# Overflow bookkeeping off GpSimd, row stores issued by ScalarE, and two token parts in one matmul operand for experts of at most 64 slots

## The chip, the cores and the metric

The kernel runs on one core of one Trainium2 chip. The metric is the device time of one execution in microseconds; for the kernel before it is 2696.34 us, the median of three runs (2691.31 to 2696.85). Times in the profile are microseconds unless marked ns. Engines: PE is TensorE (its matmuls; PEld its weight loads), DVE is VectorE, ACT is ScalarE, POOL is GpSimd, SP is SyncE, whose queue issues most DMAs.

## What is computed

Two transformer blocks on 512 tokens of width 1024, in fp32. The second block ends in a mixture of experts, the only part that the change touches:

```python
def swiglu(x, w_gu, w_down):
    g, u = jnp.split(x @ w_gu, 2, axis=-1)
    return (jax.nn.silu(g) * u) @ w_down

def moe_ffn(x2d, w_router, router_bias, w_exp_gu, w_exp_down, w_sh_gu, w_sh_down):
    scores = jax.nn.sigmoid((x2d @ w_router).astype(jnp.float32))
    sel = scores + router_bias.astype(jnp.float32)
    ...
    _, top_idx = lax.top_k(sel, TOP_K)
    w = jnp.take_along_axis(scores, top_idx, axis=1)
    w = w / jnp.sum(w, axis=-1, keepdims=True) * ROUTED_SCALE
    ...
    def expert_block(args):
        tok, e = args
        return swiglu(x_pad[tok], w_exp_gu[e], w_exp_down[e])
    ...
    routed = jnp.zeros((T + 1, D), x2d.dtype).at[buf_tok].add(out)[:T]
    return routed + swiglu(x2d, w_sh_gu, w_sh_down)
```

There are 64 experts. Each has a gate-and-up weight of 1024x512 and a down weight of 256x1024, 3 MB together. One shared expert works on all tokens. A layer norm follows.

## The kernel before

**fp32 by parts.** An fp32 operand is split into a high part and the rest: `split` (L216) copies with rounding to fp32r on ACT and subtracts on DVE. A product takes three matmuls, `mm3` (L192 to L194): high by high, high by low, low by high. Weights are split the same way when they have landed: units of 128x2048, copy on ACT (`unit<-whole`, `unit<-unit`), subtraction on DVE.

**Routing.** `route` computes the router's scores on PE, a sigmoid on ACT (L1623), the choice of groups and of experts on DVE (L1625 to L1690), and each expert's list of tokens. The experts are then worked off by falling count, each with a fixed number of slots, its cap (`CAPS`): 34 experts have caps of 66 to 104, and the 30 last ones 64 or fewer (5 of 64, 9 of 60, 5 of 56, 6 of 52, 5 of 48). The token rows are copied by POOL into tiles `xr` (two buffers) and stored by SP to the DRAM tensor `xr_d`, four stores of 128 rows (L1532), from which the experts gather.

**The loop over experts.** Iteration e, in the order in which the code issues it: POOL gathers the rows of expert e+4 from `xr_d` (indirect DMA, L1833); the gate-and-up weights of e+1 are split; `up(e)` does 24 matmuls of 512 columns, then silu on ACT (L1859) and the product on DVE (L1860); the down weight of e is split; `turn(e+1)` transposes the gathered rows on PE (L1847, 8 transposes) and splits them into `gh` and `gl`; `down(e-1)` does 12 matmuls, then two scaled copies into `ey` on ACT (L1877, two buffers), and POOL adds `ey` to the rows of the DRAM tensor `acc_d` by an indirect DMA that accumulates (the scatter, L1879); SP issues the weight loads of later experts; `turn_mid(e)` transposes the product (L1865) and splits it into `ehh` and `ehl`. Slot lists for later experts are made between (L1779 to L1786). Each scatter waits for the one before, as both add to `acc_d`.

**Order of the instructions.** A scheduler that works from the data dependences and its own costs orders the instructions of each engine when the kernel is built; each engine then runs its list in order.

**Overflow.** An expert with more tokens than its cap gets further blocks after the loop. `overflow()` makes the list of those blocks and runs in steps, one in each iteration from e = 8 on: a row of cap bounds by 75 memsets on POOL (L1740), comparisons and a scan on DVE, and three lists, for which a tile `cs` is filled by an iota on POOL (L1753), then by copies on ACT.

## Time and profile before

| | |
|---|---|
| median of 3 runs | 2696.34 us |
| the profiled execution, its own time | 2697.15 us |
| its span in the trace | 2695.4 us |
| mean granted clock of TensorE, of full speed | 0.974 |
| PE busy | 2532.2 us, 94% |
| DVE busy | 1983.9 us, 74% |
| ACT busy | 1439.6 us, 53% |
| POOL busy | 497.7 us, 18% |
| read from and written to HBM | 405.70 MB and 41.60 MB |

The span is the time between the first and the last instruction in the trace; the run's own time holds a little more. The mixture of experts begins at about 1900 us: routing and the shared expert to about 1982, the experts with caps above 64 to about 2360, the others to about 2670, then the final layer norm. A busy share tells how much an engine does, not whether anything waits for it; the idle time in brackets behind an instruction of a timeline, with what ended it, tells that.

### The profile page before, as it was taken

To read this page: it belongs to the slowest core of one execution; us is meant where nothing else is said; L and a number is where in the kernel's file an instruction comes from. 1 tells how busy PE (TensorE), PEld (TensorE's weight loads), DVE (VectorE), ACT (ScalarE), POOL (GpSimd) and SP (SyncE) were. 2 spreads that over 40 slices of the span, in tenths; PEclk is the share of its full clock that TensorE was granted. 3 is DMA by queue.
4 is the path that set the end of the run, shared out by engine and by line. 5 is a ranking of instruction groups with operands and counts; after the bars stand their busy time and mean duration, and the time that the engine had idled before them with its cause. 6 is when DMAs were issued, how large, how long until landed. Compare 5 with 4: busy or idle time off the path is not lost. (4 is left out here: it accounts for less than half of the span.)

```text
span 2695.4 us, 33112 instructions
## 1 busy us (share of the span) xinstructions
PE 2532.2 (94%) x12188; PEld 1929.2 (72%) x12188; DVE 1983.9 (74%) x2921; ACT 1439.6 (53%) x1874; POOL 497.7 (18%) x606
## 2 busy tenths in 40 slices
PE   8999999999998888999999999999889899999995
PEld 6778878888887676888888777788666565555552
DVE  6987865763667985763756798757679788888885
ACT  6656443432433564432434566535348677777783
POOL 0212200000002210000000347000214344434332
PEclk9999999999999898999999999999889899999997
DMA  4334332323223101223224632533569999999994
GB/s 135 126 110 125 106 126 85 106 79 108 94 82 106 32 32 63 94 83 105 95 84 126 189 113 88 198 121 132 228 202 331 319 354 346 355 358 365 362 360 147
DMA packets 232969, 449.49 MB, mean 167 GB/s; under 512 B 23375, under 2 KB 172815, under 8 KB 207205
## 3 DMA queue, kind: packets, MB, share of 16 engines
q1 hardware_dynamic: 220677, 410.42, 44.4%
q0 software_dynamic: 12128, 36.94, 5.9%
q8 instruction: 97, 1.59, 0.2%
q14 instruction: 67, 0.55, 0.1%
HBM read 405.70 MB, written 41.60 MB: 166 GB/s over the span
## 5 line engine op out<-in xcount | busy, mean ns | idle before, releaser
L192 PE MATMUL acc<-xh,unit 128*128 128x512 f32 (+1 forms) x1584 | 623.9, 394 | 4.8 <-ACT unit L216 1.8
L193 PE MATMUL acc<-xl,unit 128*128 128x512 f32 (+1 forms) x1584 | 624.0, 394 | 0.0
L194 PE MATMUL acc<-xh,lower 128*128 128x512 f32 (+1 forms) x1576 | 620.1, 394 | 0.0
L216 DVE TENSOR_TENSOR lower<-whole,unit 128x2048 fp32r<-128x2048 f32 (+3 forms) x218 | 463.6, 2127 | 210.5 <-ACT unit L216 210.0
L216 ACT ACTIVATE unit<-whole 128x2048 fp32r<-128x2048 f32 (+3 forms) x223 | 397.3, 1782 | 345.8 <-DMA whole<-in_f_down_w_dram 116.2
L192 PEld LDWEIGHTS acc<-xh,unit 128*128 128x128 f32 (+1 forms) x1584 | 297.6, 188 | 69.1 <-ACT unit L216 2.3
L193 PEld LDWEIGHTS acc<-xl,unit 128*128 128x128 f32 (+1 forms) x1584 | 297.9, 188 | 62.3 <-DVE xl L276 0.6
L194 PEld LDWEIGHTS acc<-xh,lower 128*128 128x128 f32 (+1 forms) x1576 | 296.3, 188 | 62.9 <-issue 2.3
L216 DVE TENSOR_TENSOR unit<-unit 128x2048 fp32r<-128x2048 f32 x131 | 298.5, 2285 | 30.0 <-ACT unit L216 27.2
L216 ACT ACTIVATE unit<-unit 128x2048 fp32r<-128x2048 f32 x131 | 249.0, 1913 | 26.5 <-PE acc L194 9.1
L1879 POOL DMA_INDIRECT acc_d<-ey,idx x64 | 148.2, 2316 | 353.0 <-DMA acc_d<-ey,idx 77.5
L192 PE MATMUL acc<-unit,gh 128*60 128x512 f32 (+14 forms) x512 | 208.1, 406 | 3.1 <-ACT gh L216 1.9
L194 PE MATMUL acc<-unit,gl 128*60 128x512 f32 (+14 forms) x512 | 208.1, 406 | 1.7 <-DVE gl L216 1.6
L311 DVE SCALAR_TENSOR_TENSOR y<-u,vtab,y 128x510 f32<-128x510 f32 (+1 forms) x176 | 131.2, 749 | 29.7 <-ACT y L309 25.3
L194 PE MATMUL acc<-mh,lower 128*128 128x512 f32 x352 | 138.7, 394 | 0.0
L192 PE MATMUL acc<-mh,unit 128*128 128x512 f32 x352 | 138.7, 394 | 0.0
L193 PE MATMUL acc<-ml,unit 128*128 128x512 f32 x352 | 138.7, 394 | 0.0
L1833 POOL DMA_INDIRECT xg<-xr_d,idx x64 | 105.5, 1649 | 106.6 <-PE aux L1847 53.3
L624 DVE SCALAR_TENSOR_TENSOR cc<-gg,vtab,cc 128x512 f32<-128x512 f32 x148 | 119.9, 868 | 1.1 <-ACT cc L594 1.0
L193 PE MATMUL acc<-unit,gh 128*60 128x512 f32 (+14 forms) x288 | 116.8, 405 | 0.0
L192 PE MATMUL acc<-unit,ehh 128*60 128x512 f32 (+14 forms) x256 | 101.1, 408 | 12.5 <-ACT ehh L216 12.4
L1877 ACT ACTIVATE ey<-acc,slot 60x512 f32<-60x512 f32 (+13 forms) x128 | 84.1, 681 | 51.9 <-PE acc L194 23.4
(691 smaller groups left out, 4555.7 us busy)
## 6 DMA issues: line engine op xcount, KB each, us to landing
unit<-in_w_exp_gu_dram SPq DMA_DIRECT2D x72, 1024.0 KB
unit<-in_w_exp_down_dram SPq DMA_DIRECT2D x59, 1024.0 KB
whole<-in_w_exp_gu_dram SPq DMA_DIRECT2D x56, 1024.0 KB
whole<-in_f_up_w_dram SPq DMA_DIRECT2D x44, 1024.0 KB
whole<-in_a_in_proj_dram SPq DMA_DIRECT2D x16, 1024.0 KB
whole<-in_f_down_w_dram SPq DMA_DIRECT2D x16, 768.0 KB
whole<-in_b_pw_w_dram SPq DMA_DIRECT2D x12, 1024.0 KB
whole<-in_w_in_dram SPq DMA_DIRECT2D x12, 1024.0 KB
```

Of the source, the lines that this page charges most:

```text
L192: T.matmul(ps, lhsT=ah, rhs=bh, start=start, stop=False)
L193: T.matmul(ps, lhsT=ah, rhs=bl, start=False, stop=False)
L194: T.matmul(ps, lhsT=al, rhs=bh, start=False, stop=stop)
L216: return A.activation(out=xh, in_=x, func=AF.Copy), eng.tensor_sub(xl, x, xh.bitcast(F32))
L311: V.scalar_tensor_tensor(y[:, d:], in0=u[:, :S - d], scalar=vcol(cw, (2 - d) * 44 + j), in1=y[:, d:], op0=ALU.mult, op1=ALU.add)
L624: V.scalar_tensor_tensor(c, in0=gg[j][:, k:k + S], scalar=vcol("b_dw_w", k * KD + j), in1=c, op0=ALU.mult, op1=ALU.add)
L1833: self.gathered = G.indirect_dma_start(out=self.xg, out_offset=None, in_=xr_d, in_offset=IO(ap=self.idx, axis=0))
L1877: A.activation(out=y[:, n0:n0 + S], in_=ps, func=AF.Copy, scale=self.wgt)
L1879: G.indirect_dma_start(out=acc_d, out_offset=IO(ap=self.idx, axis=0), in_=y, in_offset=None, compute_op=ALU.add)
```

## The change

Three parts. (1) The four stores to `xr_d` are issued by ACT's queue and no longer by SP's. (2) `overflow()` uses no GpSimd step and no copies: the caps stand in a constant tile `caps`, filled by 15 memsets at the start of the kernel; adding the bound of a block and comparing go into one DVE operation for each of five blocks; the list of experts' numbers comes from the constants `irow` and `eids`, broadcast. (3) `gh` and `gl` become two places in one tile `gs`. For experts with cap at most 64, `gl` starts at column 64, and `up()` multiplies both at once: for each of the 8 slices of the inner dimension one matmul with 64+cap stationary columns against the high part of the weight and one with cap columns against the low part, 16 instead of 24. The result of the low tokens stands in the rows from 64 on; ACT copies it to a new tile `gx`, DVE adds the other rows to it, and silu and product read `gx`. Where cap is under 64 (25 experts), POOL clears the columns between.

```diff
@@ -1529,7 +1529,7 @@
                     xr = turned.tile([P, D], F32, name="xr", tag="gb", bufs=2)
                     G.tensor_copy(xr.rearrange("p (u k q) -> p u k q", u=2, k=4),
                                   xn[:, t, :].rearrange("p (u q k) -> p u k q", u=2, k=4))
-                    nc.sync.dma_start(out=xr_d[1 + t * P:1 + (t + 1) * P, :], in_=xr)
+                    nc.scalar.dma_start(out=xr_d[1 + t * P:1 + (t + 1) * P, :], in_=xr)
                 shared(rp, xn, acc_d, sh, last)
             dense.close()
             free_units[:] = [p for p in free_units if p is not wp]
@@ -1568,7 +1568,7 @@
                         for i, x in enumerate((a["ln3_g_2"], a["ln3_b_2"])):
                             nc.sync.dma_start(out=ln3[:, i * D:(i + 1) * D], in_=x[0].partition_broadcast(P))
                     if e >= OVERFLOW_AT:
-                        steps = steps or overflow(sp, mb, ob, pcol, eids, n_more, more, ex[e].gathered)
+                        steps = steps or overflow(sp, mb, ob, pcol, eids, n_more, more)
                         next(steps, None)
 
                 g3, b3 = (ln3[:, i:i + D] for i in (0, D))
@@ -1723,40 +1723,34 @@
                 V.tensor_sub(wm, wm, rr[:, :, :, i])
         return posm, rr, mb, ob, pcol, eids
 
-    def overflow(sp, mb, ob, pcol, eids, n_more, more, gathered):
+    def overflow(sp, mb, ob, pcol, eids, n_more, more):
 
         n = N_OVER * NE
-        room = sp.tile([P, 4 * n + P + 1], F32, name="room", bufs=1)
-        bv, fl, hit, cs = (room[:, i * n:(i + 1) * n] for i in range(4))
-        dg, lst = room[:, 4 * n:4 * n + P], room[:, 4 * n + P:4 * n + P + 1]
+        room = sp.tile([P, 3 * n + P + 1], F32, name="room", bufs=1)
+        fl, hit, cs = (room[:, i * n:(i + 1) * n] for i in range(3))
+        dg, lst = room[:, 3 * n:3 * n + P], room[:, 3 * n + P:3 * n + P + 1]
 
         def blocks(x):
             return x.rearrange("p (b e) -> p b e", e=NE)
 
-        with tc.issue_after(gathered.ins):
-            for e in range(NE):
-                if e == 0 or CAPS[e] != CAPS[e - 1]:
-                    for b in range(N_OVER):
-                        G.memset(blocks(bv)[:, b, e:], float(CAPS[e] + b * CAP))
         pc = aux([P, NE])
         for t in range(NT):
             T.matmul(pc, lhsT=ob, rhs=mb[:, t, :], start=t == 0, stop=t == NT - 1)
         for b in range(N_OVER):
-            V.tensor_tensor(blocks(fl)[:, b, :], blocks(bv)[:, b, :], pc, op=ALU.is_lt)
+            V.scalar_tensor_tensor(blocks(fl)[:, b, :], in0=caps, scalar=float(b * CAP), in1=pc, op0=ALU.add, op1=ALU.is_lt)
         yield
         V.tensor_scalar(hit, fl, 0.0, 1.0, op0=ALU.mult, op1=ALU.add)
         V.tensor_tensor_scan(cs, hit, fl, 0.0, op0=ALU.mult, op1=ALU.add)
         V.tensor_copy(n_more, cs[:, n - 1:])
         V.scalar_tensor_tensor(hit, in0=cs, scalar=pcol, in1=fl, op0=ALU.is_equal, op1=ALU.mult)
         for i in range(3):
-            if i == 0:
-                G.iota(blocks(cs), pattern=[[0, N_OVER], [1, NE]], base=0, channel_multiplier=0,
-                       allow_small_or_imprecise_dtypes=True)
-            if i == 1:
+            yield
+            if i < 2:
+                V.tensor_mul(blocks(fl), blocks(hit), (irow[:, :NE], eids)[i][:, None, :].to_broadcast([P, N_OVER, NE]))
+            else:
                 for b in range(N_OVER):
-                    copy(blocks(cs)[:, b, :], eids)
-            yield
-            V.tensor_mul(fl, bv if i == 2 else cs, hit)
+                    V.scalar_tensor_tensor(blocks(fl)[:, b, :], in0=caps, scalar=float(b * CAP), in1=blocks(hit)[:, b, :],
+                                           op0=ALU.add, op1=ALU.mult)
             V.reduce_sum(lst, fl, axis=AX.X)
             V.tensor_scalar(dg, ident, lst, None, op0=ALU.mult)
             yield
@@ -1765,6 +1759,10 @@
             V.tensor_copy(more[i], pl)
             yield
 
+    caps = const.tile([P, NE], F32, name="caps")
+    for e in range(NE):
+        if e == 0 or CAPS[e] != CAPS[e - 1]:
+            G.memset(caps[:, e:], float(CAPS[e]))
     irow = const.tile([P, P], F32, name="irow")
     G.iota(irow, pattern=[[1, P]], base=0, channel_multiplier=0, allow_small_or_imprecise_dtypes=True)
     pad = const.tile([P, 1], F32, name="pad")
@@ -1839,25 +1837,44 @@
             self.dn = cut(self.unit[2], self.turned)
 
         def turn(self):
-            self.gh = self.gp.tile([P, KD, CAP], F32R, name="gh", tag="gh", bufs=2)[:, :, :self.cap]
-            self.gl = self.gp.tile([P, KD, CAP], F32R, name="gl", tag="gl", bufs=2)[:, :, :self.cap]
+
+            cap = self.cap
+            self.wide = cap <= 64
+            at = 64 if self.wide else CAP
+            self.gs = self.gp.tile([P, KD, 2 * CAP], F32R, name="gs", tag="gs", bufs=2)
+            self.gh, self.gl = self.gs[:, :, :cap], self.gs[:, :, at:at + cap]
+            if self.wide and cap < 64:
+                G.memset(self.gs[:, :, cap:64].bitcast(F32), 0.0)
             for k4 in range(0, KD, 4):
-                pt = aux([P, 4, self.cap])
+                pt = aux([P, 4, cap])
                 for k in range(4):
-                    T.transpose(pt[:, k, :], self.xg[:, (k4 + k) * P:(k4 + k + 1) * P], ident[:self.cap, :self.cap])
+                    T.transpose(pt[:, k, :], self.xg[:, (k4 + k) * P:(k4 + k + 1) * P], ident[:cap, :cap])
                 self.turned = split(self.gh[:, k4:k4 + 4, :], self.gl[:, k4:k4 + 4, :], pt)
 
         def up(self):
-            ps = bank()[:self.cap]
+            cap = self.cap
+            ps = bank()
             for k in range(KD):
                 hi, lo = w = self.gu[k // 4]
-                mm3(ps, self.gh[:, k, :], self.gl[:, k, :], hi[:, k % 4, :], lo[:, k % 4, :], k == 0, k == KD - 1)
+                if self.wide:
+                    both = [(64 + cap, hi), (cap, lo)]
+                    for n, x in both if k == 0 else both[::-1]:
+                        T.matmul(ps[:n], lhsT=self.gs[:, k, :n], rhs=x[:, k % 4, :], start=k == 0 and x is hi,
+                                 stop=k == KD - 1 and x is hi)
+                else:
+                    mm3(ps[:cap], self.gh[:, k, :], self.gl[:, k, :], hi[:, k % 4, :], lo[:, k % 4, :], k == 0, k == KD - 1)
                 if k % 4 == 3:
                     free(w)
-            self.hx = self.sp.tile([CAP, 256], F32, name="hx", tag="hx", bufs=2)[:self.cap]
+            if self.wide:
+                x = self.sp.tile([64, S], F32, name="gx", tag="gx", bufs=1)[:cap]
+                copy(x, ps[64:64 + cap])
+                V.tensor_add(x, x, ps[:cap])
+            else:
+                x = ps[:cap]
+            self.hx = self.sp.tile([CAP, 256], F32, name="hx", tag="hx", bufs=2)[:cap]
             by_block = self.hx.rearrange("t (k p) -> t p k", k=2)
-            A.activation(out=by_block, in_=ps[:, 0:256].rearrange("t (p k) -> t p k", k=2), func=AF.Silu)
-            V.tensor_mul(by_block, by_block, ps[:, 256:512].rearrange("t (p k) -> t p k", k=2))
+            A.activation(out=by_block, in_=x[:, 0:256].rearrange("t (p k) -> t p k", k=2), func=AF.Silu)
+            V.tensor_mul(by_block, by_block, x[:, 256:512].rearrange("t (p k) -> t p k", k=2))
 
         def turn_mid(self):
             pt = aux([P, 2, self.cap])
```

What the scheduler makes of it, at two places. **Routing, ACT**, from the first copy of the router's sums (`rsc<-acc`) to the sigmoid (L1623 `rsc<-aux`); `unit<-whole` are weight copies for the shared expert and the first experts, `xh` the high part of the tokens. Before:

```order
L77 ACTIVATE rsc<-acc 64x256
L216 ACTIVATE xh<-aux 128x4x128 x2
L216 ACTIVATE unit<-whole_68 128x2048
L216 ACTIVATE unit<-whole_70 128x2048
L77 ACTIVATE rsc<-acc 64x256
L216 ACTIVATE unit<-whole_66 128x2048
L1623 ACT_TABLE_LOAD
L1623 ACTIVATE rsc<-aux 128x256
```

After:

```order
L77 ACTIVATE rsc<-acc 64x256
L1532 DMA xr_d<-xr 128x1024
L216 ACTIVATE xh<-aux 128x4x128 x2
L1532 DMA xr_d<-xr 128x1024 x2
L216 ACTIVATE unit<-whole_68 128x2048
L77 ACTIVATE rsc<-acc 64x256
L1532 DMA xr_d<-xr 128x1024
L1623 ACT_TABLE_LOAD
L1623 ACTIVATE rsc<-aux 128x256
L216 ACTIVATE unit<-whole_70 128x2048
L216 ACTIVATE unit<-whole_66 128x2048
```

The four stores stand between the copies; two of the three weight copies stand behind the sigmoid now.

**Routing, DVE**, from the last split of the tokens on; `lower` are the low parts of the weights just named, `MAX` and `gs` steps of the choice of groups. Before:

```order
L216 TENSOR_TENSOR xl<-aux,xh 128x4x128 x2
L216 TENSOR_TENSOR lower_69<-whole_68,unit 128x2048
L216 TENSOR_TENSOR lower_71<-whole_70,unit 128x2048
L216 TENSOR_TENSOR lower_67<-whole_66,unit 128x2048
L1625 TENSOR_TENSOR rsel<-rsc,rb_14551 128x256
L1630 MAX t_14554<-rsel 128x8 x32
L1632 TENSOR_TENSOR gs<-t_14554 128x32
```

After:

```order
L216 TENSOR_TENSOR lower_69<-whole_68,unit 128x2048
L1625 TENSOR_TENSOR rsel<-rsc,rb_14567 128x256
L1630 MAX t_14570<-rsel 128x8 x32
L216 TENSOR_TENSOR lower_71<-whole_70,unit 128x2048
L1632 TENSOR_TENSOR gs<-t_14570 128x32
L216 TENSOR_TENSOR lower_67<-whole_66,unit 128x2048
L1640 TENSOR_TENSOR t_14570<-gs 128x256
```

Two of the three weight subtractions moved from ahead of the choice of groups into it.

**The second expert of cap 56, PE**: the end of `down(e-1)` (`ehh`, `ehl`), `turn_mid(e)` (`ident,hx`), the slot lists (`rr,oh`), and `up(e+1)` (`gh`, `gl`, after the change `gs`). Before:

```order
L193 MATMUL acc<-unit,ehh 56x512
L194 MATMUL acc<-unit,ehl 56x512
L192 MATMUL acc<-unit,gh 56x512
L193 MATMUL acc<-unit,gh 56x512
L1865 MATMUL aux<-ident,hx 128x56 x2
L1782 LDWEIGHTS oh
L1782 MATMUL aux<-rr,oh 52x6
...
L194 MATMUL acc<-unit,gl 56x512
L192 MATMUL acc<-unit,gh 56x512
```

After:

```order
L193 MATMUL acc<-unit,ehh 56x512
L194 MATMUL acc<-unit,ehl 56x512
L1882 MATMUL aux<-ident,hx 128x56 x2
L1780 LDWEIGHTS oh
L1780 MATMUL aux<-rr,oh 52x6
...
L1862 MATMUL acc<-unit,gs 120x512
L1862 MATMUL acc<-unit,gs 56x512 x2
L1862 MATMUL acc<-unit,gs 120x512
```

`turn_mid(e)` stood two matmuls deep in `up(e+1)`, and stands ahead of it now; a matmul of 120 rows stands for two of 56.

**The same expert, ACT**: `hx` is its silu, `ey` the copies of e-1, `gh` (or `gs`) the split of e+1's rows, `unit` weight copies, `ehh` the splits of the products. Before:

```order
L216 ACTIVATE ehh<-aux 128x2x56
L216 ACTIVATE unit<-unit 128x2048
L216 ACTIVATE unit<-whole_66 128x2048
L1859 ACTIVATE hx<-acc 56x128x2
L216 ACTIVATE gh<-aux 128x4x56 x2
L1877 ACTIVATE ey<-acc,slot 56x512 x2
L216 ACTIVATE unit<-unit 128x2048
L216 ACTIVATE ehh<-aux 128x2x56
```

After:

```order
L216 ACTIVATE ehh<-aux 128x2x56
L77 ACTIVATE gx<-acc 56x512
L216 ACTIVATE unit<-unit 128x2048
L216 ACTIVATE gs<-aux 128x4x56 x2
L1894 ACTIVATE ey<-acc,slot 56x512 x2
L1876 ACTIVATE hx<-gx 56x128x2
L216 ACTIVATE unit<-unit 128x2048
L216 ACTIVATE ehh<-aux 128x2x56
```

The silu stood right behind `up(e)`; now the copy into `gx` stands there, and a weight copy, a split of e+1's rows and the two `ey` of e-1 stand between it and the silu.

## Rows read from the trace of the kernel before

**Rows 1.** Windows: stretch, length, busy us of PE, PEld, DVE, ACT, POOL, clock, DMA share, GB/s.

```profile
2365.00:2600.00 235.00, 227.54 (x1166) 126.69 (x1166) 202.23 (x258) 183.53 (x211) 87.30 (x47) 1.00 1.02 360
...
2640.00:2696.00 56.00, 22.06 (x90) 10.95 (x90) 28.09 (x36) 19.02 (x26) 14.76 (x7) 0.73 0.34 98
```

**Rows 2.** The scatters' line L1879 from 2365 to 2600: who waited (us, times), landing.

```profile
  ACT ey L1877: 13.1, 7
...
DMA to landing us min/median/max: 7.8/9.1/10.5
```

**Rows 3.** Timeline of POOL: start, us, instruction, count, idle before and its releaser.

```profile
2449.54 1.81 POOL L1879 DMA_INDIRECT acc_d<-ey,idx  x1 [6.25 <-ACT unit L216]
...
2459.63 1.47 POOL L1879 DMA_INDIRECT acc_d<-ey,idx  x1 [0.81 <-ACT ey L1877]
```

**Rows 4.** Timeline of ACT in the same stretch.

```profile
2449.42 1.25 ACT L1877 ACTIVATE ey<-acc,slot 60x512 f32<-60x512 f32 x2
...
2458.93 0.68 ACT L1877 ACTIVATE ey<-acc,slot 60x512 f32<-60x512 f32 x1 [2.06 <-DMA acc_d<-ey,idx]
```

**Rows 5.** Timeline of PE in an expert's up, 60 stationary columns.

```profile
2464.62 0.40 PE L192 MATMUL acc<-unit,gh 128*60 128x512 f32 x1
2464.85 0.39 PE L193 MATMUL acc<-lower,gh 128*60 128x512 f32 x1
```

**Rows 6.** Timeline of PE in the shared expert, at the lower clock.

```profile
1970.96 0.63 PE L192 MATMUL acc<-unit,sh 128*128 128x512 f32 x1
1971.39 0.63 PE L193 MATMUL acc<-lower,sh 128*128 128x512 f32 x1
```

**Rows 7.** Timeline of SP's queue during the routing: DMAs issued.

```profile
1923.77 2.82 SPq L1532 DMA_DIRECT2D xr_d<-xr  x2
1943.22 0.33 SPq L165 DMA_DIRECT2D whole<-in_w_exp_gu_dram  x1
```

**Rows 8.** Timeline of POOL: the row copies, then the first gather.

```profile
1944.99 4.26 POOL L1530 COPY xr<-xn 128x1024 f32<-128x1024 f32 x2 [19.41 <-DMA xr_d<-xr]
...
1965.31 1.15 POOL L1833 DMA_INDIRECT xg<-xr_d,idx  x1 [16.06 <-PE aux L1782]
```

**Rows 9.** Timeline of PE: the routing, and the end of the shared expert.

```profile
1949.55 1.03 PE L1693 MATMUL aux<-ident,rwm 128*64 128x128 f32 x4 [2.26 <-DVE rwm L1663]
...
1981.33 0.39 PE L193 MATMUL acc<-lower,sh 128*128 128x512 f32 x1
1981.56 0.39 PE L194 MATMUL acc<-unit,sh 128*128 128x512 f32 x1
1981.79 0.82 PE L1847 MATMUL aux<-ident,xg 96*128 96x96 f32 x8
```

**Rows 10.** The gathers' line L1833, whole run: landing.

```profile
DMA to landing us min/median/max: 4.2/9.6/13.6
```

**Rows 11.** Timeline of DVE in the overflow steps.

```profile
2107.69 0.49 DVE L1759 TENSOR_TENSOR room<-room 128x320 f32<-128x320 f32 x1 [9.99 <-POOL room L1753]
```

**Rows 12.** Timeline of POOL: the overflow's memsets, and scatters around its iota.

```profile
2030.30 4.98 POOL L1740 MEMSET room<- 128x64 f32 x75
...
2105.65 1.54 POOL L1879 DMA_INDIRECT acc_d<-ey,idx  x1 [8.43 <-DMA acc_d<-ey,idx]
...
2116.26 2.29 POOL L1879 DMA_INDIRECT acc_d<-ey,idx  x1 [7.22 <-DMA acc_d<-ey,idx]
```

**Rows 13.** Lines of ACT, 2365 to 2600: busy us, mean ns, idle before and releasers.

```profile
L216 ACT ACTIVATE unit<-unit 128x2048 fp32r<-128x2048 f32 x46 | 87.2, 1909 | 1.1 <-PE aux L1782 1.1
...
L1859 ACT ACTIVATE hx<-acc 60x256 f32<-60x256 f32 (+3 forms) x24 | 15.2, 632 | 22.1 <-PE acc L194 22.0
```

**Rows 14.** Lines of DVE in the same stretch.

```profile
L216 DVE TENSOR_TENSOR lower<-whole,unit 128x2048 fp32r<-128x2048 f32 x24 | 54.8, 2282 | 2.2 <-ACT unit L216 2.2
...
L1860 DVE TENSOR_TENSOR hx<-hx,acc 60x256 f32<-60x256 f32 (+3 forms) x24 | 14.7, 611 | 3.1 <-ACT hx L1859 3.1
```

**Rows 15.** Lines of DVE, shapes apart, 1965 to 2700: an add of 128x512.

```profile
L1809 DVE SCALAR_TENSOR_TENSOR xn<-xn,acc 128x512 f32<-128x512 f32 x8 | 5.4, 686 | 3.1 <-PE acc L194 3.1
```

**Rows 16.** Timeline of POOL: the last two scatters.

```profile
2661.75 1.34 POOL L1879 DMA_INDIRECT acc_d<-ey,idx  x1 [5.86 <-ACT ehh L216]
2666.78 1.34 POOL L1879 DMA_INDIRECT acc_d<-ey,idx  x1 [3.69 <-DMA acc_d<-ey,idx]
```

## The prediction, made before the changed kernel was run

> **What bounds the kernel now.** The change touches the MoE stage only, so I first cut that stage into stretches in the view of windows. In the stretch of the wide experts (cap at most 64; e = 34 to 63, of which 24 fall into it) PE is busy 227.54 of 235.00 us, 97%, at clock 1.00, while the DMA engines show a share of 1.02 at 360 GB/s [rows 1]. Both look like a bound, and only one can be relaxed by the change. 235 us over 24 experts is about 10 us each.
>
> So I asked what releases the last step of an expert, the scatter-accumulate into acc_d on POOL. They run one after another: the one at 2449.54 lands when ScalarE is released at 2458.93 by "DMA acc_d<-ey,idx", and the next starts at 2459.63 [rows 3, 4], 10.1 us after the first. The landing takes 7.8 to 10.5 us, median 9.1, in this stretch [rows 2]. With 0.8 us from landing to start that is 9.9 us an expert, the cadence seen. The data of the second scatter was ready long before: its two ey instructions end at 2449.42 + 1.25 = 2450.67, 9 us ahead of it [rows 4]. ey has two buffers, so ScalarE, running ahead, meets the scatter of two experts earlier: 13.1 us of its idle time in 7 places [rows 2]. PE is busy 97%, but **the chain of scatters under a full DMA load sets the period**; PE has a lead of 8 to 9 us that it can't use up. At the end, after the last weights have landed (DMA share 0.34 in the last stretch [rows 1]), the scatters come as compute delivers them: 2661.75 waits 5.86 us for ScalarE's ehh [rows 16].
>
> **The change part by part.**
>
> *Fewer matmuls (30 experts).* N=512 matmuls start 0.23 us apart at full clock (2464.62, 2464.85 [rows 5]). Those have 60 stationary columns; the shared FFN's with 128 start 0.23 apart as well (1981.33, 1981.56 [rows 9]), so I take the same for 64+cap. 24 become 16: 8 x 0.231 = 1.85 us less PE per expert, 55 us in all. In return comes a gx copy on ScalarE (as ey, 0.68 [rows 4]), an add on DVE (128x512: 0.686 [rows 15]), and ahead of silu and product (0.632 and 0.611 [rows 13, 14]) they make the way from up to turn_mid 1.4 us longer. The order also moves turn_mid(e) ahead of up(e+1) in about 19 of the 30, where it stood among the first matmuls of up(e+1). Then PE does after up(e): transposes 0.7 and down(e-1) 12 x 0.231 = 2.8, together 3.5 us, before it needs the product. If ScalarE has silu right after gx, that needs 0.69 + 0.69 + 0.63 + 0.61 = 2.6: no wait, and the loop is 16 x 0.231 + 2.8 + 0.7 + 0.6 (turn_mid, slots) = 7.8. If the ey of e-1 stand before silu, as the order has it in 24 of 30 with one at least, these end after down, at 4.2, and the product at 5.5: PE waits 2.0, loop 9.8. With a weight split (1.909 [rows 13]) ahead of it as well, in about 14, 11.7. The mean is near 9.8 against 9.65 in the same hand count before, both under the 9.9 of the scatter chain. So the 55 us are **returned as idle time of PE: net 0** in the wide stage, bounds -55 (PE the bound after all) to +10 (the second rival).
>
> The memset of the columns cap to 64 (25 experts) goes to POOL behind a scatter that waits; the next use is the turn of the same expert, 3 to 5 us later by the order in which the scatters stood: 0.
>
> *Overflow.* Before, DVE sat 9.99 us idle at 2107.69 until POOL's iota, itself queued behind the scatter of 2105.65 [rows 11, 12]. After, no GpSimd step stands there. But the scatters around it are 2105.65 and 2116.26, 10.6 us apart [rows 12], not 20, since the lead of ey paid for it: what the chain lost is 0.7 us here, and up to the whole 9.99 if the next ones were held up. I take -3. The 75 memsets, 4.98 us at 2030.30 with a scatter queued behind them [rows 12], go away: -1 (bounds 0 and -4.98), since the chain of scatters was young and had little lead there. Fifteen memsets of the same kind come at the kernel's start, where POOL waits: 0. For both together 0 to -10, cover and full stall; -4 lies nearer to the 0.7 that the spacing shows.
>
> *Row stores on ScalarE's queue.* Before, SP issues the first two at 1923.77 behind nine weight loads, and POOL's third xr copy waits for their landing: 19.41 us idle up to 1944.99 [rows 7, 8], 21.2 us from the issue. On ScalarE they stand before silu's work of the shared FFN and the sigmoid of the router, and stores 3 and 4 need POOL copies 3 and 4, which need the landings of 1 and 2 (xr has two buffers). So ScalarE, in order, is blocked from store 2 (about 1925.6) until copy 3 is done; behind it are three weight splits, one rsc copy and the sigmoid. The landing on its own queue isn't in the trace: between 4.2 (fastest gather) and 21.2; the median of the gathers, which run on their own queue beside the weight loads, is 9.6 [rows 10], and I take that. Store 1 from about 1922.5 lands at 1932.1, copy 3 ends at 1934.1; store 2 lands at 1935.3, copy 4 at 1937.4, so the sigmoid comes some 4 us later than before. On DVE two weight splits (2.28 each, [rows 14]) now stand between the router's steps: together up to 8.5 us on the route. PE waited for that route, 2.26 us at 1949.55 [rows 9]. The first gather at 1965.31 needs 6 us and its transposes start only at 1981.79, after the shared FFN [rows 8, 9]: 10 us of cover for the route itself, not for the shared FFN's weight splits that are blocked with it. An issue takes SP 0.33 us [rows 7]; four on ScalarE 1.3, which lie in its wait. I take +3, bounds 0 (all covered) to +14 (21.2 us landing).
>
> The Trainium skill, "DMA: Bandwidth & Descriptors", section "Queues, rings and completion order", says that a DMA engine takes turns between the queue rows it has work for, a packet at a time; so a store on ScalarE's row need not stand behind the loads on SP's. By that the term would be at the low end, 0 to +3; the trace agrees for the gathers on POOL's row (4.2 to 13.6 us to landing [rows 10]), and no run shows it for ScalarE's.
>
> *Tail.* Scatters 2661.75 and 2666.78 close the stage [rows 16]. With the last two up() shorter by 1.85 each (3.7) and one gx chain longer by 1.4: -2. The chain of landings (5.0 from 2661.75 to 2666.78) allows -6 at most; +3 if silu stands behind ey there.
>
> **Sum.** Against the profiled execution's own 2697.15 us: +3 - 4 + 0 - 2 = -3, 2694 us. (That execution lies 0.8 us above the median of the runs, which span 5.5 us.)
>
> **Rivals.**
> 1. *Everything covered*: the start costs nothing, overflow gives 6, the tail 6: 2685 us. For it: 10 us of cover at the first gather [rows 8, 9]. Against: ScalarE is blocked in front of the shared FFN's splits too. 0.28.
> 2. *The longer way through an expert* (slower): the loop of the wide experts is not 9.8 but 10.6, because silu stands behind ey, which itself waits for the scatter of two experts before, and behind a weight split. It decides once the loop is above 9.9: 0.6 x 30 = 18 us over the chain's pace, less the lead of 8: +10, with start and overflow -1 and no tail gain, 2706 us. For it: DVE and ScalarE are at 202 and 184 of 235 already [rows 1]. Against: the loops by hand come to 9.8. 0.18.
> 3. *PE is the bound*: if landings shorten with the pace, all 55 us come off: 2642 us. For it PE's 97%; against it the DMA share of 1.02 and the 9 us for which finished ey waits [rows 1, 4]. 0.06.
> 4. *Row stores land as late as on SP's queue*, 21 us: start +14, 2697 + 14 - 6 = 2705 us. 0.06.
> 5. *PE's clock falls* once it idles a fifth of the stage. At 1.2 GHz a matmul starts each 0.43 us (1970.96, 1971.39 [rows 6]) instead of 0.23: 28 x 0.2 = 5.6 us an expert; five such experts less the lead of 8 give +20, 2713 us. The clock was 0.73 in the last stretch, where PE is busy 22.06 of 56 us, and 1.00 in the wide stage [rows 1]. 0.04. The Trainium skill, "TensorE: Matmul & The Clock Gate", section "What's actually happening", calls the slow state the default that activity lifts; that agrees with those two rows, and no run here shows it for 78% busy.
>
> **How the numbers follow.** Forecast within 0.2% of before (about what a measurement can tell from no change, 5.4 us): 0.38, at 2694. Faster: rivals 1 and 3 are 0.34. Slower: 2, 4 and 5 are 0.28. The range takes in rivals 1, 2 and 4 with some spread on the two outer ones, 2680 to 2709, leaving out 3, 5 and the outer part of 2. The likeliest case's own range is 2690 to 2700.
>
> **What would show it.** Right: PE's busy share in the wide stretch falls to some 78%, clock 1.00, the scatters still 10 us apart with landings near 9, DMA share still 1.0. DVE has no idle time near 10 us in the overflow steps. ScalarE shows some 8 us of idle time before store 3, released by POOL's copy. Wrong: scatters less than 9.5 us apart (rival 3), scatters released by ScalarE's ey rather than by landings (rival 2), matmul cadence of 0.43 in the wide stage (5), or a matmul with 120 columns that takes more than 0.231.

## The result, and the profile after the change

The changed kernel takes 2712.84 us (median of 4 runs, 2711.62 to 2714.15) against 2693.82 of the kernel before beside it: **1.0068, 95% interval 1.0045 to 1.0091**, slower by some 18 us. The forecast was 2694, the range 2680 to 2709; both missed. The profiled execution took 2714.15 us, its span is 2712.4.

The windows of the changed kernel, columns as in [rows 1]:

```profile
2365.00:2600.00 235.00, 191.39 (x901) 115.72 (x900) 198.55 (x259) 183.60 (x216) 122.41 (x63) 0.90 0.96 338
...
2640.00:2712.00 72.00, 36.06 (x156) 19.95 (x155) 45.58 (x51) 34.61 (x45) 19.85 (x12) 0.76 0.51 165
```

PE is busy 191 us of 235, about as the missing matmuls would have it. But two columns moved that I had expected to stand: the clock, 1.00 before, is 0.90, and the DMA share, 1.02 before, is 0.96, at 338 GB/s where it had been 360. The DMA view of the same 235 us, each digit a fortieth of the stretch, shows the difference as gaps. Of the kernel before:

```profile
DMA  9999999999999999999999999999999999999999
...
DMA packets 13889, 84.57 MB, mean 360 GB/s; under 512 B 2197, under 2 KB 2197, under 8 KB 4954
```

Of the changed kernel:

```profile
DMA  9999898999999799999969998999997999999995
...
DMA packets 12917, 79.41 MB, mean 338 GB/s; under 512 B 2005, under 2 KB 2005, under 8 KB 4457
```

5.16 MB less were moved in the same time; at 360 GB/s that is 14 us of transfers that came later. What PE waits for, from 2365 to 2640 (us, times, longest), in the kernel before:

```profile
PE acc L192 <- ACT ehh L216: 4.2, 7, 1.4
PE aux L1865 <- DVE hx L1860: 3.8, 3, 1.7
```

and in the changed one:

```profile
PE aux L1882 <- DVE hx L1877: 40.7, 24, 4.1
PE acc L1862 <- DVE gs L216: 8.5, 4, 5.7
```

41 us of waiting for the product in turn_mid, in 24 of the experts, where it was 4.

How a wait of PE becomes a gap of the DMA engines can be read at one place, the first wide experts, from four timelines. ACT:

```profile
2372.41 1.92 ACT L216 ACTIVATE unit<-unit 128x2048 fp32r<-128x2048 f32 x1 [4.38 <-DMA unit<-in_w_exp_down_dram]
2374.23 0.66 ACT L1894 ACTIVATE ey<-acc,slot 66x512 f32<-66x512 f32 x1
2374.80 0.26 ACT L216 ACTIVATE ehh<-aux 128x128 fp32r<-128x128 f32 x1
```

DVE:

```profile
2375.09 0.29 DVE L216 TENSOR_TENSOR ehl<-aux,ehh 128x128 fp32r<-128x128 f32 x1 [4.68 <-ACT ehh L216]
...
2376.12 4.48 DVE L216 TENSOR_TENSOR unit<-unit 128x2048 fp32r<-128x2048 f32 x2
2380.53 2.28 DVE L216 TENSOR_TENSOR lower<-whole,unit 128x2048 fp32r<-128x2048 f32 x1
2382.73 0.67 DVE L1871 TENSOR_TENSOR gx<-gx,acc 64x512 f32<-64x512 f32 x1
2383.33 0.74 DVE L216 TENSOR_TENSOR gs<-aux,gs 128x256 fp32r<-128x256 f32 x2
```

PE, and SP's queue:

```profile
2383.79 2.08 PE L1862 MATMUL acc<-unit,gs 128*128 128x512 f32 x4 [5.68 <-DVE gs L216]
...
2388.26 0.63 PE L1862 MATMUL acc<-lower,gs 128*64 128x512 f32 x1
2388.69 0.63 PE L1862 MATMUL acc<-unit,gs 128*128 128x512 f32 x1
```

```profile
2378.53 0.34 SPq L165 DMA_DIRECT2D unit<-in_w_exp_gu_dram  x1
2390.98 0.33 SPq L165 DMA_DIRECT2D whole<-in_w_exp_gu_dram  x1
```

ACT waits 4.38 us for a down weight; behind it stands ehh, for which DVE waits 4.68; behind that stand three weight subtractions and gx's add, 7.4 us, ahead of the split of the next expert's rows, for which PE waits 5.68; then PE runs at the lower clock (0.43 us from one matmul to the next at 2388). Only when up() has read its weights are their buffers free, and for 12.45 us SP issues no load; from 2390 to 2392 the DMA share is 0.75, at 193 GB/s. Nothing here is long; each engine does its list in order, and PE is no longer far enough behind the others for that to be hidden.

What SP's queue waits for from 2365 to 2640 (us, times, longest), before and then after:

```profile
SPq L165 <- PE acc L194: 185.9, 26, 10.0
```

```profile
SPq L165 <- PE acc L1862: 186.2, 25, 11.9
```

The sum is the same and the longest wait is not. Counted from the packets under way at each moment, the DMA engines stand idle for 1.1 us of these 275 before, as a mean of the 16, and for 13.6 after. Of the 13.6, 11.5 lie in six places where 11.8 to 12.6 us pass between two loads on SP, and in the 2.5 us behind each; before, no such stretch is longer than 10.4 us until the last load. In five of the six PE waits 3.2 to 4.1 us for the product, in the sixth, the one shown, 5.7 us for the split rows.

### The profile page after: what moved, and what is told of

Same layout as the page of the kernel before. It is cut to its first block, busy times and chain, and to the rows that moved or that the text cites. A ratio compares the mean times of both kernels' runs of the same rounds, so it can differ in the third digit from the quotient of the medians.

```text
span 2712.4 us, 32762 instructions
## 1 busy us (share of the span) xinstructions
PE 2499.1 (92%) x11948; PEld 1922.6 (71%) x11948; DVE 1999.6 (74%) x2955; ACT 1460.3 (54%) x1899; POOL 522.1 (19%) x570
## 5 line engine op out<-in xcount | busy, mean ns | idle before, releaser
L1831 POOL DMA_INDIRECT xg<-xr_d,idx x64 | 130.3, 2035 | 97.6 <-PE aux L1851 37.2
L1862 PE MATMUL acc<-unit,gs 128*124 128x512 f32 (+9 forms) x360 | 130.6, 463 | 14.2 <-DVE gs L216 12.9
L192 PE MATMUL acc<-unit,gs 128*70 128x512 f32 (+9 forms) x272 | 111.5, 410 | 2.4 <-ACT gs L216 2.3
L194 PE MATMUL acc<-unit,gs 128*70 128x512 f32 (+9 forms) x272 | 110.7, 407 | 2.6 <-DVE gs L216 2.5
```

Of the source, the lines that this page charges most:

```text
L192: T.matmul(ps, lhsT=ah, rhs=bh, start=start, stop=False)
L194: T.matmul(ps, lhsT=al, rhs=bh, start=False, stop=stop)
L1831: self.gathered = G.indirect_dma_start(out=self.xg, out_offset=None, in_=xr_d, in_offset=IO(ap=self.idx, axis=0))
L1862: T.matmul(ps[:n], lhsT=self.gs[:, k, :n], rhs=x[:, k % 4, :], start=k == 0 and x is hi, stop=k == KD - 1 and x is hi)
```

## The experiments

Three numbers help to compare the kernels, since executions of one and the same code reach the mixture of experts anywhere from 1915 to 1928 us into the span (the part ahead of it has the same instructions in all). From each trace: **to last weight**, from the first copy of the router's sums (`rsc<-acc` on ACT) to the end of the last packet of expert weights; **gaps**, the time in which a DMA engine has no packet, as a mean of the 16, between the same two points, counted from the packets under way at each moment; **difference**, the one less the other; **tail**, from the end of that packet to the end of the span. Ratios are against the kernel before, run beside. The names: p1, p2, p3 and p12 have parts of the change; nogx is without gx, gx24 has gx and 24 matmuls; silu, hard30 and hard31 have a fixed order at one or two places; warm has matmuls that fill idle time, warm0 is its control; acc2 and sum have two tensors for the scatters; _b repeats a kernel. The columns behind the ratio are of one execution each; two of one kernel differ in them by up to 3.5 us.

| kernel | ratio (95%) | to last weight | gaps | difference | tail |
|---|---|---|---|---|---|
| before | 1 | 720.4 | 37.2 | 683.2 | 54.9 |
| changed | 1.0068 (1.0045 to 1.0091) | 729.4 | 46.2 | 683.2 | 56.1 |
| p1 | 1.0008 (0.9994 to 1.0021) | 718.2 | 35.9 | 682.3 | 54.8 |
| p2 | 0.9988 (0.9972 to 1.0003) | 714.1 | 34.9 | 679.2 | 54.0 |
| p12 | 1.0002 (0.9990 to 1.0014) | 713.6 | 32.9 | 680.7 | 56.1 |
| p3 | 1.0072 (1.0058 to 1.0086) | 733.5 | 47.1 | 686.4 | 57.4 |
| gx24 | 1.0063 (1.0041 to 1.0084) | 740.8 | 52.7 | 688.1 | 57.7 |
| nogx | 1.0067 (1.0046 to 1.0088) | 727.3 | 43.7 | 683.6 | 59.8 |
| nogx_b | 1.0067 (1.0042 to 1.0092) | 723.8 | 41.1 | 682.7 | 62.1 |
| nogx30 | 1.0058 (1.0039 to 1.0077) | 726.3 | 43.3 | 683.0 | 62.1 |
| silu | 1.0030 (1.0018 to 1.0041) | 724.6 | 43.7 | 680.9 | 55.2 |
| hard30 | 1.0010 (0.9995 to 1.0026) | 718.6 | 34.7 | 683.9 | 54.7 |
| hard31 | 1.0018 (1.0006 to 1.0029) | 714.6 | 34.1 | 680.5 | 55.8 |
| warm0, warm0_b | 1.0029 (1.0006 to 1.0052), 1.0020 (1.0007 to 1.0033) | 727.8, 725.5 | 41.5, 38.1 | 686.3, 687.4 | 53.2, 52.4 |
| warm, warm_b | 1.0012 (0.9995 to 1.0029), 1.0019 (1.0001 to 1.0037) | 716.6, 713.9 | 33.8, 33.5 | 682.8, 680.4 | 57.1, 55.9 |
| p12_acc2 | one run | 707.6 | 28.0 | 679.6 | 48.3 |
| hard31_acc2 | one run | 713.8 | 29.5 | 684.3 | 51.4 |
| p12_sum | 1.0000 (0.9985 to 1.0016) | 711.2 | 30.8 | 680.4 | 61.0 |

The column "difference" is the finding: **in all of them the DMA engines need 679 to 688 us for this work, and what moves the end of the stage is how long they stand idle.** The end of the kernel moves by the tail besides.

**Which part of the change.** Each part alone, and the first two together.

```diff
p12:  - self.wide = cap <= 64
      + self.wide = False
p3:   before.py with turn() and up() of the changed kernel
p1:   - nc.sync.dma_start(out=xr_d[...], in_=xr)
      + nc.scalar.dma_start(out=xr_d[...], in_=xr)
p2:   p12 with the four row stores on nc.sync again
```

> The change without its third part for all experts: 24 matmuls in every up(), no gx; the row stores on ScalarE and the overflow steps without GpSimd stay (gh and gl stay halves of one tile). Theory 'long way' (the loss is made by the wide experts alone, whose turn_mid now waits for a product that comes late): the loss of 19 us is gone and the lead that the scatters of the changed kernel had over those of before at expert 33 (4.4 us, although everything arrives 6 us later at the mixture) stays to the end: 2684 to 2690 us. Rival 'entry' (the 6 us by which the whole stage starts later in the trace of the changed kernel belong to the change, by the place of its code or the row stores): 2694 to 2702. Rival 'row stores' (blocking ScalarE is what costs): over 2700.

> The kernel before with the third part alone: 16 matmuls and gx for the experts of cap at most 64. 'Long way': silu of expert 63 comes some 18 us later than before, as in the changed kernel, and the end with it: 2708 to 2714 us, PE in the wide stage waiting about 40 us for the product. 'Row stores' or 'entry': 2688 to 2698, no change against before.

> The kernel before with the first part alone: the four row stores on ScalarE's queue. 'Long way': within 3 us of before, since silu of expert 0 came as much later in the changed kernel as the whole stage did, 5.9 against 6.3 us: 2691 to 2697. 'Row stores': ScalarE waits 8.2 us in front of a weight split, 2700 or more.

> The change with the second part alone: overflow steps without GpSimd (row stores on SP, 24 matmuls everywhere, gh and gl halves of one tile). 'Long way': the stall of 20 us between the silus of experts 9 and 10 becomes 10, and a part of it reaches the end: 2684 to 2690. If the lead of the scatters had covered that stall wholly: 2692 to 2695.

p3 alone has the whole loss (1.0072, 2714.18 us), and PE in it waits 41.3 us for the product; p1, p2 and p12 are not told apart from before. p12 was to be at 2684 to 2690 and came to 2693.65: the lead of its scatters did not reach the end. p2, 2692.39, came where the lead covers the stall wholly, not at 2684 to 2690. "Entry" and "row stores" fall: p12's trace reaches the mixture of experts at 1920.2 us, that of before at 1920.1.

**The way through gx.** Without it, then with it and the 24 matmuls.

```diff
nogx, nogx_b:
-                x = self.sp.tile([64, S], F32, name="gx", tag="gx", bufs=1)[:cap]
-                copy(x, ps[64:64 + cap])
-                V.tensor_add(x, x, ps[:cap])
+                x = ps[:cap]
gx24 (from p12, for cap <= 64):
+                x = self.sp.tile([64, S], F32, name="gx", tag="gx", bufs=1)[:cap]
+                copy(x, ps[:cap])
+                V.tensor_tensor(x, x, ps[:cap], op=ALU.max)
```

> The changed kernel without the copy into gx and the add: silu and product read the first cap rows of the matmuls' result, so the part of the low tokens times the high weights is left out of the result. 16 matmuls for the wide experts stay. 'Long way' (PE waits for the product because gx's copy and add, and what stands ahead of the silu on ScalarE, make it late): PE waits for the product under 10 us in all in the wide stage, the silus of experts 36 to 58 are 10.0 us apart, time as without the third part, 2688 to 2696 us. 'Clock' (PE, with less to do, falls to the lower clock and that costs): PE idles as much or more, the period stays above 10.3, 2703 or more. 'PE is the bound': period near 8, under 2660.

> The changed kernel with 24 narrow matmuls for all experts, but the wide ones still pass through gx: a copy of the result on ScalarE and, in place of the add, a maximum of the copy and the result on DVE, which has the same operands and changes no value. The scheduler puts turn_mid(e) two to 20 matmuls deep into up(e+1) here, where the changed kernel has it ahead of up(e+1) in most experts. If the length of the way alone makes the loss, wherever turn_mid stands: the loop grows by 1.4 to 2 us over 9.65, period 11 or more, 2720 us or more. If place and length together make it ('long way' as I hold it): the first matmuls of up(e+1) cover the wait, period 10.0 to 10.3, 2692 to 2704 us. 'Clock': PE is busy, clock 1.00, no loss.

Both missed. Without gx the kernel is as slow as with it (1.0067; repeated, 1.0067), so the longer way is not needed for the loss. A part of it is lost at another place, though: the silus of experts 33 and 58 are 257.4 and 258.6 us apart, against 270.0 with gx, but the next five experts take longer (56.5 and 60.0 us, against 50.8), and the tail is 4 to 6 us longer; no run shows why. The rival 'clock' had nogx right, with a period of 10.31 us and 2713.48 us; it is tested below. With gx and a full list of matmuls it is slow too (1.0063; period of the silus of experts 36 to 58 10.86 us), below the 11 of length alone and above the 10.3 of place and length, although PE waits only half as much. It does not part the way's length from ScalarE's order: at least one ey of e-1 stands ahead of the silu of e for 23 of the 30 wide experts in it, as in the changed kernel, and for none before the change or in nogx. PE's wait in gx24:

```profile
PE aux L1883 <- DVE hx L1878: 20.2, 18, 2.6
```

In nogx_b the DVE timeline shows how the product comes late without gx: the silu is done at 2517.7, and the product stands behind two weight subtractions.

```profile
2518.02 2.28 DVE L216 TENSOR_TENSOR unit<-unit 128x2048 fp32r<-128x2048 f32 x1
2520.23 2.28 DVE L216 TENSOR_TENSOR lower<-whole,unit 128x2048 fp32r<-128x2048 f32 x1
2522.43 0.59 DVE L1875 TENSOR_TENSOR hx<-hx,acc 56x256 f32<-56x256 f32 x1
```

**The order.** turn_mid(e) deeper in up(e+1), the ey behind the silu, and both, each by an edge, an added dependence that fixes which of two instructions comes first. The edges hold for all 64 experts.

```diff
hard30, hard31 (up(e+1) calls turn_mid(e) behind its slice k == 3):
+                if k == 3 and between:
+                    between(m)          # m: the last matmul
...
+            with tc.issue_after(after.ins) if after else ExitStack():
                 for k in range(2):
                     T.transpose(pt[:, k, :], ...)
silu, hard31 (in down(e-1), after: the silu of e):
+                with tc.issue_after(after.ins) if after else ExitStack():
                     A.activation(out=y[:, n0:n0 + S], in_=ps, func=AF.Copy, scale=self.wgt)
```

> The changed kernel, complete, with two edges more in the order: turn_mid(e) stands a third to a half deep in up(e+1) (behind its first four slices), and the two ey of e-1 stand behind the silu of e on ScalarE. 'Long way': PE's waits for the product fall from 41 us to under 10 in the wide stage, period 10.0 by the scatters or the DMA engines, 2686 to 2696 us. 'Clock': the period stays over 10.3, 2703 or more. If the weights' and scatters' DMA were no bound: period 8.5, near 2650.

> The changed kernel with the second of these edges alone: the two ey of e-1 stand behind the silu of e, turn_mid(e) stays ahead of up(e+1) in most experts. 'Long way': the product comes 2.6 to 4.9 us after up(e), with or without a weight split ahead of the silu or the product, against 3.5 us of work that PE has: waits of 15 to 25 us in all, period 10.1 to 10.3, 2696 to 2706 us. If ScalarE's order has no part in it: 2710 to 2715.

> The changed kernel with turn_mid(e) behind the first four slices of up(e+1), and ScalarE's order left to the scheduler (ey may stand ahead of the silu). If the place of turn_mid is what counts: as with both edges (hard31), 1.001 to 1.002 of before, PE's waits for the product under 10 us in the wide stage. If ScalarE's order counts as much: 1.004 or more, and waits for the product over 15 us.

Each edge takes back a part: ey behind the silu about half (1.0030), the place of turn_mid nearly all (1.0010), both about as much (1.0018). The second is not the work of turn_mid's place alone: with this edge the scheduler also put both ey behind the silu for 21 of the 30 wide experts, where it is 7 in the changed kernel. In silu PE still waits 40.8 us for the product, not the 15 to 25 I wrote. hard31's 2702.36 us beside 2698.14 lies over the 2686 to 2696 I wrote, but its loss is under a third of the change's. PE's waits in hard30 from 2365 to 2640:

```profile
PE acc L1862 <- DVE gs L216: 33.8, 18, 4.6
PE acc L1862 <- ACT unit L216: 6.2, 2, 4.6
```

PE still waits 44 us in all, against 52 in the changed kernel, only elsewhere: for the split of the next expert's rows. Yet the DMA engines moved 84.34 MB from 2365 to 2600, nearly what they did before. So **the sum of PE's waits does not decide; what decides is whether they hold up the loads**. In nogx30, the same edge without gx, they do again:

```diff
nogx30 (from hard30):  gx left out as in nogx
```

> The changed kernel without the copy into gx and the add (the low tokens times the high weights are left out) once more. If the way through gx is not needed for the loss: 1.005 or more of before again. If the first measurement was disturbed and gx makes the loss: 1.000 to 1.002.

> The same without gx, and turn_mid(e) stands behind the first four slices of up(e+1). If the place of turn_mid makes the loss with or without gx: 1.000 to 1.002 of before, DMA share 1.01 or more in the wide stage. If other parts of the order that the scheduler made for the shorter PE list make it: 1.004 or more.

```profile
PE acc L1862 <- DVE gs L216: 14.2, 13, 4.0
PE acc L194 <- DVE ehl L216: 11.0, 8, 4.1
PE acc L1862 <- POOL gs L1847: 8.8, 2, 5.9
```

Three other waits have taken its place, one of them for the memset on POOL that I had costed at nothing. Its tail is 6 us longer as well. No single wait is the cause. Of the 8.9 us for which its DMA engines stand idle from 2365 to 2640, 8.5 lie in and right behind two stretches without a load, 13.3 us from 2497.39 and 12.4 us from 2512.76, and one of 13.7 us comes just ahead of them; hard30 has three such stretches, of 11.8 to 12.9 us and 60 us or more apart, and loses 1.5 us in them. That fits a reserve of queued loads that one stretch uses up and that needs time to come back; no run tests it.

**The clock.** Eight matmuls of constants fill PE's wait ahead of turn_mid(e); the control has nearly the same order without them (an ey ahead of the silu for 14 of the 30 wide experts, 12 with the filling).

```diff
warm, warm_b (control warm0, warm0_b: range(0)):
+            if between and self.wide:
+                for _ in range(8):
+                    after = T.matmul(ps[:64]..., lhsT=ones_r[:, :64], rhs=ones_r..., start=True, stop=True)
+            after = between(after)          # turn_mid(e-1), then the real matmuls
```

> The control for the next one: the changed kernel with the order fixed so that turn_mid(e) stands ahead of all matmuls of up(e+1) for every wide expert. 'Clock' and 'waits' alike: much as the changed kernel, PE waits for the product 30 to 50 us in the wide stage, some 70 of the 700 matmuls of 512 columns between the silus of experts 33 and 58 start 0.43 us apart (78 in the changed kernel), period 10.3 to 10.5, 2703 to 2713 us.

> As the one before, and ahead of each turn_mid(e) of a wide expert PE does eight matmuls more, of constants, whose result is overwritten: 8 x 0.231 = 1.85 us of work in the place where it waits. 'Clock' (the waits alone would fit into the 10.05 us that the DMA engines take for an expert, but they let the clock fall to 1.2 GHz and the matmuls behind them take 15 us more in all): clock 0.98 or more, hardly any matmul at 0.43 us, loop 7.8 + 1.85 + some tenths, period 10.0 to 10.1, 2692 to 2700 us although PE does more. 'Waits' (the way from up to turn_mid sets the loop whatever the clock): period stays at 10.3 to 10.5, 2703 us or more.

> The control kernel again (turn_mid ahead of all of the next up for every wide expert), for a narrower interval beside the next one on the same chip: 1.003 of before, 2702 us if before is 2695.

> The kernel with eight idle-filling matmuls ahead of each turn_mid of a wide expert again. If the fallen clock is part of the loss: 4 to 8 us under the control in time, 1.000 to 1.001 of before, although PE does 240 matmuls of 512 columns more. If it is not: equal to the control within 2 us or slower.

Windows of warm0_b, then of warm_b:

```profile
2365.00:2600.00 235.00, 199.17 (x979) 118.74 (x978) 212.00 (x276) 200.04 (x235) 113.33 (x69) 0.94 1.02 358
```

```profile
2365.00:2600.00 235.00, 229.79 (x1155) 135.31 (x1154) 211.11 (x278) 201.59 (x232) 120.94 (x68) 1.00 1.01 360
```

The filling does what it should: clock 1.00, no matmul at 0.43 us between the silus of experts 33 and 58 (56 and 80 in the two controls), waits for the product 7.1 us instead of 40.7, and gaps of 33.5 to 33.8 us instead of 38.1 to 41.5. The times hardly follow: 2700.82 against 2702.74 us, then 2698.33 against 2700.85, 2 us each time with intervals that overlap, under the 4 to 8 I had written. By the ratios it is 0.0017 and 0.0001. No cost of the 240 useless matmuls can be seen; that the clock is a part of the loss is not shown. It is not excluded either: from the first copy of the router's sums to the end, the two traces with filling take 773.7 and 769.8 us, the controls 781.0 and 777.9. The controls too are nearer to before than the changed kernel, though turn_mid stands ahead of up(e+1) in them and PE waits 41 us; in their order the silu stands ahead of both ey in more experts (16 of 30, against 7).

**One chain of scatters, or the DMA engines.** Odd experts add to a second tensor.

```diff
p12_acc2, hard31_acc2:
+        acc_2 = dram.tile([NR, D], F32, name="acc_2")
-                        ex[e - 1].down(acc_d, ...)
+                        ex[e - 1].down((acc_d, acc_2)[(e - 1) % 2], ...)
p12_sum also:
+                    V.tensor_add(y, y, y2s[t])      # y2s: the rows of acc_2
```

> The change without its third part, and the scatters of odd experts go to a second DRAM tensor of zeros, whose sum is left out of the output: two chains of scatters in place of one. My prediction said that the one chain sets the 10.05 us of an expert. If so, PE is the next bound and the period from silu 36 to silu 58 falls to 9.65 to 9.75. If the DMA engines' throughput is the bound (all 16 are busy with 36 matmuls' worth of weights, 3.6 MB an expert at 360 GB/s): 10.0 to 10.1 as before, and ey waits 9 us less for its scatter.

> The same two chains in the changed kernel with the two edges (turn_mid a third deep in up, ey behind the silu), where PE's loop without waits is some 8 us. Chain of scatters as the bound: period 8.5 to 9.3. DMA engines as the bound: 10.0 to 10.25 as with one chain.

> Parts one and two of the change, without part three, and two tensors for the scatters (odd experts add to a second one of zeros), now complete: four loads of 512 KB and four adds of 128x1024 on VectorE more before the final norm. If the one chain of scatters cost only at the end of the stage (about 6 us: the last scatters then follow compute and not each other's landing) and the sum gives back 1 to 3 of it: 2688 to 2692 us, 0.996 to 0.999 of before. If the load and the sum cost as much as the chain: 2693 to 2698.

In p12_acc2 the scatters no longer follow each other's landing; in its POOL timeline one starts at 2446.98 and the next, into the other tensor, at 2455.00, released by its own ey and 8.0 us later, where a landing takes 8.6 us at least:

```profile
2446.98 1.46 POOL L1900 DMA_INDIRECT acc_d<-ey,idx  x1 [1.35 <-ACT ehh L216]
2451.36 1.64 POOL L1835 DMA_INDIRECT xg<-xr_d,idx  x1 [2.92 <-DMA acc<-ey,idx]
2455.00 1.46 POOL L1900 DMA_INDIRECT acc<-ey,idx  x1 [2.01 <-ACT ey L1898]
```

And the pace is the same: from the silu of expert 33 to that of 58 251.4 us, in p12 251.8; 254.6 in hard31_acc2 against 258.5 with one chain, where PE's loop is near 8 by the hand count. The windows of p12_acc2, then of hard31_acc2:

```profile
2365.00:2600.00 235.00, 229.69 (x1170) 127.29 (x1170) 202.08 (x254) 185.84 (x210) 94.08 (x47) 1.00 1.02 364
```

```profile
2365.00:2600.00 235.00, 198.63 (x981) 114.80 (x980) 213.36 (x277) 199.81 (x233) 103.38 (x67) 0.96 1.02 360
```

In p12_acc2 PE is busy 98% of the time, so this run alone does not tell PE from the DMA engines as the bound. hard31_acc2 does: PE is idle 15% there, the DMA share is 1.02, and the period of 10.1 us is the one expected if the DMA engines are the bound (10.0 to 10.25), not if it was the chain (8.5 to 9.3). So the chain was not the bound. At the end it costs some 1 us: the last scatter starts 25.7 us after the last weight in p12_acc2, 26.8 in p12. That the tail is 48.3 us instead of 56.1 is for the rest because the norm, with the sum left out, does not wait for that scatter. The 2672.79 us of that one run have three sources, beside the trace of p12: an early start (1915), 5 us less of gaps, and this tail. With the sum the tail is 61.0 us, as the rows of both tensors have to be loaded and added before the norm, and p12_sum stands at 1.0000: 2688 to 2692 was wrong. None of the kernels with an interval beats the one before beyond it.

## Why the prediction was wrong, point by point

- **"The chain of scatters under a full DMA load sets the period": wrong, and the step that failed first.** The DMA share of 1.02 stood in the same row [rows 1] and was named as the second candidate; I took the landing times for a cause [rows 2 to 4], and they are what a full queue looks like: they are 8.6 to 12.4 us in p12_acc2, where the scatters do not wait for one another. Two chains leave the period as it is, and in the changed kernel the chain hardly holds anything: from 2365 to 2600 one ey waits 0.2 us for a scatter, where seven waited 13.1 us [rows 2].

```profile
  ACT ey L1894: 0.2, 1
```

  With the chain as the bound the 8 to 9 us for which finished ey wait are a reserve; with the DMA engines as the bound there is none, since time that they lose is not made up.
- **"Returned as idle time of PE: net 0": the idle time is right, the net is wrong.** PE's busy share fell to 81% (78 was forecast), and a wide expert cost more, not the same: 270.0 us for 25 of them against 252.0 before and 251.8 in p12, 18 us. What I left out is that SP's loads wait for PE: from 2365 to 2640 SP's queue stood 186 us, in 25 pieces of up to 11.9, until matmuls of up() had freed their weights. Before it was 185.9 us and up to 10.0: the same sum, in pieces that the loads already queued could bridge (1.1 us of idle DMA time, 13.6 after). PE's progress is the valve of the DMA engines, so its waits are not idle time beside the bound.
- **Loop of 9.8 us by hand: mis-sized.** The prediction's own cases, 6 of 30 at 7.8 us, 10 at 9.8 and 14 at 11.7, have a mean of 10.3 and not of 9.8, and that is over the 9.9 of the chain. (In rival 2, 10.6 less 9.9 is 0.7 and not 0.6, 3 us more in all.) The silus of experts 36 to 58 are 10.47 us apart in the changed kernel, near the 10.6 of rival 2, and the step from 33 to 36 adds 9 us (39.8 against 31.0). Rival 2 is the mechanism that came, a later product behind ey and weight work on in-order engines; it had 0.18. Its price of 2706 us lies 7 under the 2713 measured, about the 8 us of lead that I subtracted. Its reason, the longer way, is not the whole of it: the loss is there without gx as well.
- **Rival 5, the clock: there, its cost open.** The clock fell to 0.90 in the wide stage, and 78 of some 700 matmuls started 0.43 us apart, 15.6 us of PE's time. I had given it 0.04 as an event. That it costs time is not shown (2 us, within the intervals). Its 2713 us meet the measured time, but by luck as far as the runs tell: it took five experts wholly at the lower clock, 28 us, and gx24 loses as much as the changed kernel with a clock of 0.97 from 2365 to 2640 and 35 such matmuls.
- **Row stores, +3: no cost.** From the first copy of the router's sums to silu 0 it is 69.0 us before, 68.2 after and 68.4 in p1. The steps were as worked out, the cover was larger. POOL, then ACT with its queue, in the changed kernel:

```profile
1938.63 1.97 POOL L1530 COPY xr<-xn 128x1024 f32<-128x1024 f32 x1 [6.42 <-DMA xr_d<-xr]
```

```profile
1929.00 0.35 ACTq L1532 DMA_DIRECT2D xr_d<-xr  x1
...
1941.01 1.91 ACT L216 ACTIVATE unit<-whole 128x2048 fp32r<-128x2048 f32 x1 [8.22 <-DMA xr_d<-xr]
```

  The store of 1929.00 lets POOL's third copy go at 1938.63, 9.6 us later, the value taken from the gathers' median [rows 10]; on SP it was 21.2. The Trainium skill's rule ("DMA: Bandwidth & Descriptors", "Queues, rings and completion order"), that an engine takes turns between queue rows, agrees with that. ScalarE was blocked for 8.2 us, and nothing of it reached silu 0.
- **Overflow, -4: agrees, not clear of noise.** The silus of experts 9 and 10 are 10.5 us apart instead of 19.7, and p2 stands at 0.9988, 3 us, with an interval that touches 1. By its trace it needs 714.1 us to the last weight instead of 720.4.
- **Tail, -2: wrong.** 56.1 us from the last weight to the end, against 54.9.
- **Memset at 0: right in the changed kernel**, where nothing waits for it; in nogx30 two waits of PE, 8.8 us, end with it.

What stays open is which property of the order makes the loads late. ey ahead of the silu has a part in the changed kernel, shown by silu; hard30 shows that fixing turn_mid's place takes nearly all of the loss back, though it moves the ey as well. Without gx the same edge does not help (nogx30), with no ey ahead of the silu in it at all; the idle time of its DMA engines in the wide stage lies at one place, and what makes its stretches without a load follow one another there was not found.

## What to carry to other kernels

Where the DMA engines are busy all the time, read first what lets the loads go: the engine whose work frees their buffers is on the critical path even if a fifth of it is idle, and where it waits long enough for the queued loads to run out, the DMA engines stand idle. Taking work from the busiest engine then bought nothing here, and took away the slack behind which in-order neighbours hid their own queues. Before a saving is booked as harmless at worst, ask who had been covered by the work that goes.

## What the runs showed of the hardware

- A matmul of 512 columns starts 0.23 us after the one before with 128 as with 64 stationary columns, at full clock (2372.35, 2372.59 and 2372.82 in the changed kernel), as taken.
- PE busy 191 of 235 us had a clock of 0.90 in this kernel, and 199 of 235 one of 0.94 in warm0_b; 230 of 235 have 1.00 (warm_b). It fell behind single waits such as that of 5.68 us above, to matmuls 0.43 us apart.
- The same instructions ahead of the mixture of experts took 1915 to 1928 us in the 20 traces; a difference of a few us between two spans says nothing until it is taken from a common point.
